# Projecting three units from x split without its norm, with the token factors applied later

## The chip, the cores and the metric

The kernel runs on one NeuronCore of a Trainium2 chip. The metric is the time of one execution on the device in microseconds (us). The kernel before took 1175.54 us (median of 3 runs, 1175.41 to 1177.18).

## What is computed

One step of a hybrid decoder layer on 1088 tokens (1024 of a prompt, 8 times 8 of samples) of width 1024, in float32. Only the first lines matter for this change:

```python
h = rmsnorm(x, norm_mix_pre[l])              # x * rsqrt(mean(x*x) + eps) * g
(a_b, a_c, a_u, b_p, c_q, c_f, c_i, c_g, d_a, d_g) = jnp.split(h @ w_in[l], N_BLOCKS, axis=-1)
...
f = lb + (1.0 - lb) * jax.nn.sigmoid(zf4)    # zf is c_f, q = silu(c_q), v = c_i
...
mix = jnp.concatenate([ya, yb, yc, yd], axis=-1) @ w_out[l]
x = x + rmsnorm(mix, norm_mix_post[l])
```

The norm multiplies each token (a row of x) by one number, r(token) = rsqrt(mean(x*x) + eps), and each channel by a gain g. The factor r can be applied to x ahead of the product with `w_in` or to the product behind it.

## The kernel before, in words

All products run on TensorE as float32 split in two parts: a value is stored as a rounded high part (`xh`, `wop` slot 0) and the remainder (`xl`, `wop` slot 1), and one product is three matmuls: high by high, low x by high weight, high x by low weight. The high part is made by a copy on ScalarE (ACT), the low part by a subtraction on VectorE (DVE) that needs the high part. `XH[k]` and `XL[k]` (k = 0 to 7) hold the normed input, channels of block k on the partitions and the 1088 tokens along the row.

**Units.** The 2560 columns of `w_in` are 20 units of 128 columns. A unit is 8 blocks k times 3 token chunks `CH` (256, 384 and 448 tokens) times 3 matmuls: 72 matmuls into three PSUM banks (`mm`, six banks, so two units at a time). A unit's weights come in two halves of 256 KB (`raw`, 4 buffers), each split into `wop` (4 buffers). `UNITS` is the order of the units; a unit's handler (`c_f`, `c_q`, `c_v`, `d_gate`, ...) evacuates its banks and does the work of its mixer. Unit 10 is the forget gate zf of head pair 0 (`c_f`, sigmoid), unit 8 its query (`c_q`, silu), unit 12 its value (`c_v`); with zf and the query in SBUF the generator `hgrn(0)` can run, a long chain of DVE work with short matmul blocks on TensorE (lines L746, L759, L811 and on).

**The start.** x comes in token-major from `xn`: nine tiles, 128 tokens on the partitions and 1024 channels in the row (in the buffers `ys`, line L213). For a chunk c: ACT squares each tile with a row sum (`x_sq`, L228), DVE makes r from the sums (`x_norm`) and scales the tiles (L68, partly on GpSimd), TensorE transposes them block by block (`x_split`, L249), ACT takes the high part with the gain out of PSUM (L250) and DVE the low part (L71). Units `U0` = 10 and `U1` = 8 run chunk by chunk between these transposes (`mm_part`, L148). This start is written by hand inside a block that keeps the written order on ACT, DVE and TensorE.

**After it.** `unit` (L997) issues the other 18 units, and a budget hook puts the handlers' work between their matmuls: after every 4 or 8 matmuls it lets generators in the lists `first`, `crit` and `bulk` issue instructions until a budget of modelled work is spent. The order of the instructions on TensorE and DVE is therefore fixed when the program is built. `bulk` holds the depthwise convolutions (60 DVE instructions L71 of 128x1024), `first` the evacuations and the splits of the next unit's weights. Then follow the output projection (L1131) and the feed-forward part, which the change does not touch.

A norm by `rsqrt_steps` is 12 small DVE instructions. `bcast` (L189) turns a column of factors into the same row on all 128 partitions, by a transpose on TensorE into PSUM. `ht()` is a 1088-wide scratch tile (six of them), `zt()` one of two others.

Of the kernel before, what the change touches and what calls it, by code (L numbers as in the profile page):

```python
# [52 lines left out]
def body(ctx, tc, xn, xT, win, wout, wgu, wdn, par, con, msk, poolw, s_conv, s_pool, s_hgrn, s_conf,  # L53
# [165 lines left out]
    def x_idx(c):
        o, n = CH[c]  # L220
        return [i for i, (go, gn) in enumerate(GRP) if o <= go < o + n]

    def x_sq(c):
        ss = sst[c]
        for a, i in enumerate(x_idx(c)):
            gn = GRP[i][1]
            junk = ht(D)
            S.activation(junk[:gn], xs[i][:gn], AF.Square, accum_out=ss[:gn, a:a + 1])  # L228
            yield ss

    def x_norm(c, ss):
        idx = x_idx(c)
        args = ss[:, :len(idx)], [P, len(idx)], 1.0 / D, f"x{CH[c][1]}"
        if c == 0:
            r = rsqrt_pow(*args)
        else:
            for r in rsqrt_steps(*args):
                yield
        for a, i in enumerate(idx):
            gn = GRP[i][1]  # L240
            TS(xs[i][:gn], xs[i][:gn], r[:gn, a:a + 1], 0.0, eng=GP if c and a % 2 else V)
            yield

    def x_split(c, k):
        o, n = CH[c]
        ps = T(mmp, [P, 512], "mm") if k % 2 and c < 2 else sm()
        for i in x_idx(c):
            go, gn = GRP[i]
            PE.transpose(ps[:, go - o:go - o + gn], xs[i][:gn, k * P:(k + 1) * P], ident[:gn, :gn])  # L249
        S.activation(XH[k][:, o:o + n], ps[:, :n], AF.Copy, scale=pc("g_mix", k))  # L250
# [2 lines left out]
    with tc.manual_schedule(engines={mybir.EngineType.Activation, mybir.EngineType.DVE, mybir.EngineType.PE}):
        sq = [x_sq(c) for c in range(3)]

        def steps(g, n):
            for _ in range(n):
                next(g, None)

        for ss in sq[0]:  # L260
            pass
        steps(x_norm(0, ss), 99)
        prep_unit(U0)
        next(sq[1])
        ss1 = next(sq[1])
        x_split(0, 0)
        x_split(0, 1)
        next(sq[1])
        n1 = x_norm(1, ss1)
        pu = {u: [T(mmp, [P, 512], "mm")] for u in (U0,)}  # L270
        for k in range(2, KT):
            x_split(0, k)
            steps(n1, 3)
            mm_part(pu[U0], wq[U0], k - 2, 0)
            if k >= 5:
                ss2 = next(sq[2])
        steps(n1, 99)
        next(sq[2])
        n2 = x_norm(2, ss2)
        mm_part(pu[U0], wq[U0], 6, 0)  # L280
        mm_part(pu[U0], wq[U0], 7, 0)
        pu[U0].append(T(mmp, [P, 512], "mm"))
        pu[U1] = [T(mmp, [P, 512], "mm")]
        for k in range(KT):
            x_split(1, k)
            steps(n2, 2)
            if k == 1:
                prep_unit(U1)
            if k >= 2:
                mm_part(pu[U0], wq[U0], k - 2, 1)  # L290
            if k >= 4:
                mm_part(pu[U1], wq[U1], k - 4, 0)
        steps(n2, 99)
        for k in range(4, KT):
            if k >= 6:
                mm_part(pu[U0], wq[U0], k, 1)
            mm_part(pu[U1], wq[U1], k, 0)
        pu[U0].append(T(mmp, [P, 512], "mm"))
        pu[U1].append(T(mmp, [P, 512], "mm"))
        for k in range(KT):  # L300
            x_split(2, k)
            mm_part(pu[U1], wq[U1], k, 1)
            if k >= 2:
                mm_part(pu[U0], wq[U0], k - 2, 2)
        mm_part(pu[U0], wq[U0], 6, 2)
        mm_part(pu[U0], wq[U0], 7, 2)
        pu[U1].append(T(mmp, [P, 512], "mm"))
        load_unit(U2)
        for k in range(KT):
            mm_part(pu[U1], wq[U1], k, 2)  # L310
            if k == 2:
                prep_unit(U2)
# [1580 lines left out]
```

## Time and profile before

| | |
|---|---|
| median of 3 runs | 1175.54 us |
| the profiled execution | 1176.22 us |
| its span, first to last instruction | 1174.4 us |
| TensorE matmuls busy | 1144.4 us (97%) |
| VectorE busy | 880.8 us (75%) |
| ScalarE busy | 454.9 us (39%) |
| start, until unit three begins | 54.7 us |
| end of the projection, unit 20 | 337 us |

The profile is one execution; its span leaves out about 1.8 us of the measured time. Rows of the timeline give the start of an instruction (or of a run of equal ones), its duration and what released it. In groups the number behind the busy time is the mean duration in ns. A matmul's duration covers its way through the array, so back to back matmuls overlap: their cost on the path is the distance of their starts. "PE" is TensorE, "PEclk" the granted clock.

### The profile page before, as it was taken

The numbers are of one execution on the slowest core, as the hardware profiler recorded it, in microseconds if no ns is written. First come the engines' busy times: TensorE is split into PE (matmuls) and PEld (weight loads), VectorE is DVE, ScalarE is ACT, GpSimd is POOL, SyncE is SP. The second block draws the span as 40 slices with busy tenths as digits, with TensorE's granted clock in tenths as the row PEclk, the third lists the DMA queues.
The fourth block names the chain that finished last, engine by engine and source line by source line (L and its number), as shares of the span: only waits on it lengthen the run. The fifth ranks groups of instructions, "written<-read, shape, count | busy, mean of one in ns | idle before, by whom it ended". The sixth has DMA issues, their size and how long they took to land.

```text
span 1174.4 us, 21922 instructions
## 1 busy us (share of the span) xinstructions
PE 1144.4 (97%) x8480; PEld 1111.4 (95%) x8480; DVE 880.8 (75%) x1831; ACT 454.9 (39%) x1006; POOL 109.9 (9%) x174
## 2 busy tenths in 40 slices
PE   5999999999999999999999999999999999999995
PEld 4899899997999999999999999999999999999995
DVE  5478979996775678887667787787676668888776
ACT  7534232243274453442333444444344541123331
POOL 2100000000000000000000000000000222246323
PEclk9999999999999999999999999999999999999997
DMA  8011112211145124022331543453454687853555
GB/s 265 27 37 32 37 39 69 41 37 24 47 143 191 40 74 131 20 74 91 112 113 48 190 156 103 162 171 112 141 186 139 206 281 212 271 169 109 164 103 98
DMA packets 103401, 136.91 MB, mean 117 GB/s; under 512 B 25025, under 2 KB 72257, under 8 KB 103297
## 3 DMA queue, kind: packets, MB, share of 16 engines
q1 hardware_dynamic: 94944, 108.71, 29.5%
q0 software_dynamic: 8352, 26.81, 8.6%
q8 instruction: 66, 1.08, 0.4%
q14 instruction: 39, 0.31, 0.1%
HBM read 94.90 MB, written 40.57 MB: 115 GB/s over the span
## 4 chain that ended last, share of the span: by engine, by line
PE 92%; DVE 3%; DMA 2%; ACT 2%; issue 1%; SPq 0%; POOL 0%; ACTq 0%; DVEq 0%; POOLq 0%
PE p L1403 31%; PE mm L997 18%; PE p L1636 14%; PE p L1131 8%; PE p L1513 6%; PE p L1312 6%; PE mm L148 2%; PE sm L811 2%; DMA y<-xn 1%; DMA hx<-hi 1%; DVE wop L65 1%; PE sm L886 1%; PE p L1097 1%; PE sm L898 0%; PE sm L409 0%
## 5 line engine op out<-in xcount | busy, mean ns | idle before, releaser
L65 DVE TENSOR_TENSOR wop<-raw,wop 128x512 fp32r<-128x512 f32 (+2 forms) x296 | 195.9, 675 | 99.4 <-ACT wop L1020 90.1
L1403 PE MATMUL p<-xh,wop 128*128 128x272 f32 x1216 | 235.2, 288 | 0.6 <-DVE c L65 0.6
L1020 ACT CAST wop<-raw 128x512 fp32r<-128x512 f32 (+1 forms) x240 | 142.0, 604 | 239.3 <-DVE raw L65 120.3
L1403 PEld LDWEIGHTS p<-xh,wop 128*128 128x128 f32 x1216 | 193.3, 188 | 0.8 <-DVE c L65 0.8
L1403 PE MATMUL p<-t,wop 128*128 128x272 f32 x912 | 176.8, 288 | 0.0
L997 PE MATMUL mm<-xh,wop 128*128 128x256 f32 (+2 forms) x864 | 175.9, 331 | 0.0
L1403 PE MATMUL p<-xl,wop 128*128 128x272 f32 x608 | 175.4, 288 | 0.0
L1403 PEld LDWEIGHTS p<-t,wop 128*128 128x128 f32 x912 | 145.3, 189 | 0.0
L997 PEld LDWEIGHTS mm<-xh,wop 128*128 128x128 f32 x864 | 137.9, 188 | 5.7 <-issue 1.1
L1403 PE MATMUL p<-x,wop 128*128 128x272 f32 x456 | 130.8, 287 | 0.0
L1403 PEld LDWEIGHTS p<-xl,wop 128*128 128x128 f32 x608 | 114.4, 188 | 0.0
L1131 PE MATMUL p<-xh,wop 128*128 128x272 f32 x512 | 98.9, 290 | 0.0
L997 PE MATMUL mm<-xl,wop 128*128 128x256 f32 (+2 forms) x432 | 97.5, 333 | 0.0
L1403 PEld LDWEIGHTS p<-x,wop 128*128 128x128 f32 x456 | 86.3, 189 | 0.0
L1636 PE MATMUL p<-xh,wop 128*128 128x272 f32 x456 | 82.2, 289 | 0.0
L1636 PE MATMUL p<-xl,wop 128*128 128x272 f32 x456 | 81.5, 288 | 0.0
L1131 PEld LDWEIGHTS p<-xh,wop 128*128 128x128 f32 x512 | 81.0, 188 | 0.0
L65 DVE TENSOR_TENSOR raw<-raw,raw 128x512 f32<-128x512 f32 (+1 forms) x123 | 71.2, 589 | 10.0 <-DMA raw<-wgu 7.9
L71 DVE SCALAR_TENSOR_TENSOR y<-u,taps,y 128x1024 f32<-128x1024 f32 x60 | 77.0, 1283 | 1.6
L1131 PE MATMUL p<-xl,wop 128*128 128x272 f32 x256 | 73.9, 289 | 1.0 <-DVE xl L65 1.0
L1312 PE MATMUL p<-xh,wop 128*128 128x272 f32 x384 | 74.0, 290 | 0.0
L65 DVE TENSOR_TENSOR t<-p,t 128x272 f32<-128x272 f32 (+3 forms) x138 | 60.6, 450 | 15.9 <-PE p L1636 8.2
(323 smaller groups left out, 1997.9 us busy)
## 6 DMA issues: line engine op xcount, KB each, us to landing
raw<-wgu SPq DMA_DIRECT2D x88, 256.0 KB, 3.0
hx<-hi SPq DMA_DIRECT2D x84, 136.0 KB, 2.3
raw<-win SPq DMA_DIRECT2D x40, 256.0 KB, 2.9
hx<-x SPq DMA_DIRECT2D x64, 136.0 KB, 2.5
raw<-wdn SPq DMA_DIRECT2D x32, 256.0 KB, 3.6
xh<-hx POOLq DMA_DIRECT2D x15, 544.0 KB, 5.0
xl<-hx POOLq DMA_DIRECT2D x15, 544.0 KB, 5.2
x<-hx POOLq DMA_DIRECT2D x12, 544.0 KB, 5.0
```

Source lines behind the costliest of these rows:

```text
L65: (eng or V).tensor_tensor(out, a, b, op)
L71: (eng or V).scalar_tensor_tensor(out=out, in0=a, scalar=s, in1=b, op0=op0, op1=op1)
L148: PE.matmul(ps[c][:, :n], hl[:, wi, kk], X[k][:, o:o + n], start=k == 0 and wi == 0 and X is XH, stop=k == KT - 1 and wi == 1)
L811: PE.matmul(ps[:rows, g * P:(g + 1) * P], kk[:, o:o + rows], qz[hf][:, :, g * 64:(g + 1) * 64], start=True, stop=True, skip_group_check=True)
L886: PE.matmul(op[hs, :gn], v[:gn, g, hs], attn[:gn, g, h, :gn], start=True, stop=g == 0, skip_group_check=True)
L997: PE.matmul(ps[c][:, :w], hl[:, wi, kk], X[k][:, o:o + w], start=k == order[0] and wi == 0 and X is XH, stop=k == order[-1] and wi == 1)
L1020: S.copy(hl[:, 0], raw)
L1131: PE.matmul(ps[nt][:, :PW], WO[nt][k // 4][:, wi, kk:kk + P], X[k][:, o:o + PW], start=k == korder[0] and wi == 0 and X is XH, stop=k == k ...
L1312: PE.matmul(ps[r][:, :PW], w[:, wi, (k % 4) * P:(k % 4 + 1) * P], X[k][:, o:o + PW], start=k == 0 and wi == 0 and X is XH, stop=k == KT - ...
L1403: PE.matmul(ps[:, :PW], wop[:, wi, kk * P:(kk + 1) * P], x(kk, xi), start=first and kk == 0 and wi == 0 and xi == 0, stop=kk == 3 and wi == 1,
L1513: PE.matmul(ps[:, :n], wd[:, wi, kk * P:(kk + 1) * P], hops[k][xi][:, o:o + n], start=first and kk == 0 and wi == 0 and xi == 0, stop=not ...
L1636: PE.matmul(ps[:, :PW], ws[name][wi][q], x[:, xi, pr], start=first and q == 0 and wi == 0 and xi == 0, stop=q == 1 and wi == 1, skip_group ...
```

## The change

- x is loaded once, already transposed (`xT`, channels on the partitions), straight into `ys`; `xn`, all transposes of x and the three norms by chunk are gone.
- First split: for each k, `XH[k]` and `XL[k]` are made from x times the gain alone, in one piece of 1088 tokens (k = 0 in three), without r. The three first units (12, 10, 8 now: value, forget gate, query) run on these. Unit 12's matmuls for block k follow that block's split; those of unit 10 follow three blocks behind.
- The squares (ACT) are added up over k on DVE; nine matmuls with a column of ones give the sums per token, `rsqrt_steps` gives `r0`, and nine `bcast` with three copies give `rb0`, r spread over all partitions.
- r is applied at evacuation: unit 12 is copied out as it is and its transposed value gets r as the scale of the ACT copy (nine copies where there were three); units 10 and 8 are multiplied by `rb0` on DVE before sigmoid and silu.
- Second split, ahead of unit four (18): for each k DVE scales x in place by gain and `rb0`, ACT copies it to `XH[k]`, DVE subtracts to `XL[k]`. The other 17 units use these.
- `hgrn(0)` starts with unit four; the value's handler starts from the copy `zv`.

The diff, cut to its core:

```diff
-    UNITS = (10, 8, 12, 18, 16, 13, 19, 11, 9, 17, 4, 2, 6, 0, 5, 3, 7, 1, 14, 15)
-    U0, U1, U2 = UNITS[:3]
-    xs = [ys[i][:, :D] for i in range(KT)] + [ht(D)]
...
-                SY.dma_start(xs[i][:gn], xn[go:go + gn, :])
...
-            PE.transpose(ps[:, go - o:go - o + gn], xs[i][:gn, k * P:(k + 1) * P], ident[:gn, :gn])
-        S.activation(XH[k][:, o:o + n], ps[:, :n], AF.Copy, scale=pc("g_mix", k))
-        STT(XL[k][:, o:o + n], ps[:, :n], pc("g_mix", k), f32(XH[k][:, o:o + n]), ALU.mult, ALU.subtract)
...
+    UNITS = (12, 10, 8, 18, 16, 13, 19, 11, 9, 17, 4, 2, 6, 0, 5, 3, 7, 1, 14, 15)
+    U0, U1, U2, U3 = UNITS[:4]
+    for k in range(KT):
+        if k in (0, 2):
+            load_unit(U0 if k == 0 else U1)
+        SY.dma_start(ys[k], xT[k * P:(k + 1) * P, :])
+    load_unit(U2)
+    def split_x(k, scale, parts):
+        for o, n in parts:
+            if scale is None:
+                S.copy(XH[k][:, o:o + n], ys[k][:, o:o + n])
+                TT(XL[k][:, o:o + n], ys[k][:, o:o + n], f32(XH[k][:, o:o + n]), ALU.subtract)
+            else:
+                S.activation(XH[k][:, o:o + n], ys[k][:, o:o + n], AF.Copy, scale=scale)
+                STT(XL[k][:, o:o + n], ys[k][:, o:o + n], scale, f32(XH[k][:, o:o + n]), ALU.mult, ALU.subtract)
+    def mm_unit(n, *ks):
+        for k in ks:
+            for c in range(len(CH)):
+                mm_part(pu[n], wq[n], k, c)
...
+        prep_half(U0, 0)
+        for k in range(KT):
+            split_x(k, pc("g_mix", k), CH if k == 0 else [(0, NT)])
+            if k == 0:
+                prep_half(U0, 1)
+            if k in (2, 3):
+                prep_half(U1, k - 2)
+            sq[k] = ht(NT)
+            S.activation(sq[k], ys[k], AF.Square)
+            mm_unit(U0, k)
+            if k >= 3:
+                mm_unit(U1, k - 3)
+            if k == 1:
+                acc0 = sq[0]
+            if k >= 1:
+                TT(acc0, acc0, sq[k], ALU.add)
+        zv.append(zt())
+        for c, (o, n) in enumerate(CH):
+            S.copy(zv[0][:, o:o + n], pu[U0][c][:, :n])
+        mm_unit(U1, 5)
...
+            PE.matmul(st[:gn, i:i + 1], acc0[:, go:go + gn], ones[:, :1], start=True, stop=True, skip_group_check=True)
+        mm_unit(U1, 6)
+        for r0 in rsqrt_steps(st[:, :9], [P, 9], 1.0 / D, "x"):
             pass
+        prep_half(U2, 0)
+        prep_half(U2, 1)
+        load_unit(U3)
+        mm_unit(U1, 7)
...
+                    bcast(ps, r0[:, i:i + 1], gn, go - o)
+            S.copy(rb0[:, o:o + n], ps[:, :n])
+            mm_unit(U2, c)
+        HF[0] = ht()
+        for c, (o, n) in enumerate(CH):
+            TT(HF[0][:, o:o + n], pu[U1][c][:, :n], rb0[:, o:o + n])
+        S.activation(HF[0], HF[0], AF.Sigmoid)
+        mm_unit(U2, *range(3, KT))
+        prep_half(U3, 0)
+        prep_half(U3, 1)
         for k in range(KT):
+            STT(ys[k], ys[k], pc("g_mix", k), rb0, ALU.mult, ALU.mult)
+            split_x(k, None, [(0, NT)])
+            if k == 3:
+                HQ[0] = ht()
+                for c, (o, n) in enumerate(CH):
+                    TT(HQ[0][:, o:o + n], pu[U2][c][:, :n], rb0[:, o:o + n])
+                S.activation(HQ[0], HQ[0], AF.Silu)
...
-    free = {"h": 6, "z": 2, "u": 2, "sm": 2, "mm": 0, "v": 1, "attn": 1}
+    free = {"h": 4, "z": 1, "u": 2, "sm": 2, "mm": 6, "v": 1, "attn": 1}
...
-            S.copy(v[:n2, i:i + m], t[:n2, :m * P].rearrange("p (m c) -> p m c", c=P))
+            if ps is None:
+                for i2 in range(i, i + m):
+                    S.activation(v[:n2, i2], t[:n2, (i2 - i) * P:(i2 - i + 1) * P], AF.Copy, scale=r0[:n2, i2:i2 + 1])
+            else:
+                S.copy(v[:n2, i:i + m], t[:n2, :m * P].rearrange("p (m c) -> p m c", c=P))
```

How the instructions stand, at the two places that matter below. First DVE, where before the last chunk of x is split behind its transposes (`xl` is the low part, `sm` a transposed block in PSUM, `prm` the gains; number behind xl, xh and y is k), and behind it the splits of units two and three (`wop`):

```order
L71 SCALAR_TENSOR_TENSOR xl4_18_92<-sm_90_431,prm_1_70,xh4_10_84 128x448
L71 SCALAR_TENSOR_TENSOR xl5_19_93<-sm_91_444,prm_1_70,xh5_11_85 128x448
L71 SCALAR_TENSOR_TENSOR xl6_20_94<-sm_92_457,prm_1_70,xh6_12_86 128x448
L71 SCALAR_TENSOR_TENSOR xl7_21_95<-sm_93_470,prm_1_70,xh7_13_87 128x448
L65 TENSOR_TENSOR wop_97_503<-raw_95_490,wop_97_503 128x512
L65 TENSOR_TENSOR wop_98_506<-raw_96_492,wop_98_506 128x512
```

In the change DVE has this ahead of and in unit four, the second split (`y` is x, `h_71` is `rb0`):

```order
L65 TENSOR_TENSOR wop_76_485<-raw_66_376,wop_76_485 128x512
L65 TENSOR_TENSOR wop_77_488<-raw_67_378,wop_77_488 128x512
L71 SCALAR_TENSOR_TENSOR y0_22_102<-y0_22_102,prm_1_70,h_71_392 128x1088
L65 TENSOR_TENSOR xl0_14_88<-y0_22_102,xh0_6_80 128x1088
L71 SCALAR_TENSOR_TENSOR y1_23_103<-y1_23_103,prm_1_70,h_71_392 128x1088
L65 TENSOR_TENSOR xl1_15_89<-y1_23_103,xh1_7_81 128x1088
```

One instruction of a block moved to two, the low part standing directly behind the scaling of the same block; between the two ACT makes `xh` of that block.

Second DVE, where before `hgrn(0)` begins (`h_107` is the forget gate, `h_108` the query), while unit three runs:

```order
L68 TENSOR_SCALAR h_107_543<-h_107_543 128x1088
L65 TENSOR_TENSOR wop_115_580<-raw_112_554,wop_115_580 128x512
L65 TENSOR_TENSOR wop_116_586<-raw_113_556,wop_116_586 128x512
L723 RECIPROCAL h_117_595<-h_107_543 128x128x2
L725 RECIPROCAL h_117_595<-h_107_543 128x128
L71 SCALAR_TENSOR_TENSOR h_117_595<-h_108_547,h_117_595 128x128
```

In the change the same instructions (`h_75` the forget gate, `h_78` the query) stand among the second split of blocks 4 to 7, while unit four runs:

```order
L71 SCALAR_TENSOR_TENSOR y4_26_106<-y4_26_106,prm_1_70,h_71_392 128x1088
L68 TENSOR_SCALAR h_75_435<-h_75_435 128x1088
L65 TENSOR_TENSOR wop_96_587<-raw_90_542,wop_96_587 128x512
L65 TENSOR_TENSOR wop_97_590<-raw_91_544,wop_97_590 128x512
L715 RECIPROCAL h_99_599<-h_75_435 128x128x2
L65 TENSOR_TENSOR xl4_18_92<-y4_26_106,xh4_10_84 128x1088
L71 SCALAR_TENSOR_TENSOR y5_27_107<-y5_27_107,prm_1_70,h_71_392 128x1088
L717 RECIPROCAL h_99_599<-h_75_435 128x128
```

`hgrn(0)` moved from unit three to unit four, and its pieces now stand ahead of the low parts that unit four's matmuls need. On TensorE the blocks of `hgrn(0)` stand about 0.9 of a unit later at first, and from the tenth unit on the order is that of before.

More of the change, by code (lines that the diff above doesn't have):

```diff
@@ L50, with body @@
 NCON = 174
-def body(ctx, tc, xn, xT, win, wout, wgu, wdn, par, con, msk, poolw, s_conv, s_pool, s_hgrn, s_conf,
+def body(ctx, tc, xT, win, wout, wgu, wdn, par, con, msk, poolw, s_conv, s_pool, s_hgrn, s_conf,
          yT, o_conv_p, o_pool_p, o_hgrn_p, o_conf_p, o_conv_s, o_pool_s, o_hgrn_s, o_conf_s, hd, hx):
@@ L219, in x_idx @@
[L219 to L250, printed above, removed]
-        STT(XL[k][:, o:o + n], ps[:, :n], pc("g_mix", k), f32(XH[k][:, o:o + n]), ALU.mult, ALU.subtract)
[L253 to L260, printed above, removed]
-            pass
[L262 to L283, printed above, removed]
-        for k in range(KT):
[L285 to L312, printed above, removed]
@@ new lines, in mm_unit, with banks, prep_half @@
+    def mm_unit(n, *ks):
+        for k in ks:
+            for c in range(len(CH)):
+                mm_part(pu[n], wq[n], k, c)
+    def banks():
+        return [T(mmp, [P, 512], "mm") for _ in CH]
+    def prep_half(n, h):
+        hl = T(wp, [P, 2, 4 * P], "wop", F32R).rearrange("p w (k c) -> p w k c", c=P)
+        split_w(wraw[n][h], hl)
+        wq.setdefault(n, []).append(hl)
+    pu = {}
+    HF, HQ, zv = {}, {}, []
+    with tc.manual_schedule(engines={mybir.EngineType.Activation, mybir.EngineType.DVE, mybir.EngineType.PE}):
+        sq, acc0 = {}, None
+        pu[U0], pu[U1] = banks(), banks()
+        prep_half(U0, 0)
[18 more added lines that the diff above has]
+        mm_unit(U1, 5)
+        st = sm()
+        V.memset(st[64:, 8:9], 1.0)
+        for i, (go, gn) in enumerate(GRP):
+            PE.matmul(st[:gn, i:i + 1], acc0[:, go:go + gn], ones[:, :1], start=True, stop=True, skip_group_check=True)
+        mm_unit(U1, 6)
+        for r0 in rsqrt_steps(st[:, :9], [P, 9], 1.0 / D, "x"):
+            pass
+        prep_half(U2, 0)
+        prep_half(U2, 1)
+        load_unit(U3)
+        mm_unit(U1, 7)
+        pu[U2] = banks()
+        rb0 = ht(NT)
+        for c, (o, n) in enumerate(CH):
+            ps = sm()
+            for i, (go, gn) in enumerate(GRP):
+                if o <= go < o + n:
+                    bcast(ps, r0[:, i:i + 1], gn, go - o)
[8 more added lines that the diff above has]
+        prep_half(U3, 1)
+        for k in range(KT):
+            STT(ys[k], ys[k], pc("g_mix", k), rb0, ALU.mult, ALU.mult)
+            split_x(k, None, [(0, NT)])
+            if k == 3:
+                HQ[0] = ht()
+                for c, (o, n) in enumerate(CH):
+                    TT(HQ[0][:, o:o + n], pu[U2][c][:, :n], rb0[:, o:o + n])
+                S.activation(HQ[0], HQ[0], AF.Silu)
@@ L677, in c_v @@
     def c_v(j, ps):
-        yield from take(z=1)
-        z = zt()
-        evac(ps, z)
-        give(mm=3)
+        if ps is None:
+            z = zv[0]
+        else:
+            yield from take(z=1)
+            z = zt()
+            evac(ps, z)
+            give(mm=3)
         yield from wait(2 * LW)
@@ L693, in c_v @@
             n2 = GRP[i][1]
[L694 removed]
+            if ps is None:
+                for i2 in range(i, i + m):
+                    S.activation(v[:n2, i2], t[:n2, (i2 - i) * P:(i2 - i + 1) * P], AF.Copy, scale=r0[:n2, i2:i2 + 1])
+            else:
+                S.copy(v[:n2, i:i + m], t[:n2, :m * P].rearrange("p (m c) -> p m c", c=P))
             give(sm=1)
@@ L1053, in body @@
             if n in pu:
-                first.append(handler(j, pu[n]))
-                if i == 1:
-                    until(lambda: free["mm"] >= 3)
+                if n == U0:
+                    first.append(c_v(0, None))
+                elif n == U2:
+                    crit.append(hgrn(0))
                 continue
@@ L1871 @@
     wdn = c(a["w_down"][0].reshape(NF, P, KT, P).transpose(2, 1, 0, 3))
-    ins = {"xn": c(x), "xT": c(x.T), "win": units(a["w_in"][0]), "wout": units(a["w_out"][0]), "wgu": wgu, "wdn": wdn,
+    ins = {"xT": c(x.T), "win": units(a["w_in"][0]), "wout": units(a["w_out"][0]), "wgu": wgu, "wdn": wdn,
            "par": c(np.concatenate(par, axis=1)),
```

8 lines of the change are left out of this document (1 added, 7 removed).

## The prediction

> **What bounds the kernel now.** First the page, then TensorE's (PE's) waits, then the windows.
>
> ```profile
> span 1174.4 us, 21922 instructions
> PE 1144.4 (97%) x8480; PEld 1111.4 (95%) x8480; DVE 880.8 (75%) x1831; ACT 454.9 (39%) x1006; POOL 109.9 (9%) x174
> ```
> ```profile
> PE sm L249 <- DVE y L68: 10.5, 2, 10.3
> PE mm L148 <- ACT xh L250: 2.1, 3, 1.5
> ```
> ```profile
> 0.00:54.70 54.70, 39.85 (x217) 34.16 (x218) 26.19 (x70) 35.21 (x61) 9.23 (x16) 1.00 0.46 152
> 54.70:81.60 26.90, 26.90 (x186) 24.99 (x185) 18.32 (x35) 8.74 (x14) 0.00 (x0) 1.00 0.12 40
> 81.60:100.00 18.40, 18.40 (x126) 17.70 (x125) 12.78 (x26) 7.93 (x18) 0.00 (x0) 1.00 0.09 29
> 100.00:120.00 20.00, 20.00 (x137) 19.13 (x136) 18.82 (x31) 10.36 (x27) 0.00 (x0) 1.00 0.15 34
> 120.00:140.00 20.00, 20.00 (x134) 17.83 (x133) 18.14 (x22) 6.23 (x22) 0.00 (x0) 1.00 0.16 54
> 140.00:160.00 20.00, 20.00 (x137) 18.20 (x136) 19.38 (x24) 6.83 (x18) 0.00 (x0) 1.00 0.10 29
> 160.00:180.00 20.00, 20.00 (x133) 19.10 (x132) 13.51 (x24) 4.04 (x7) 0.10 (x1) 1.00 0.13 28
> ```
>
> PE is the bound: its columns are full from 54.7 on. Only the start lacks work for it: 14.9 of 54.7 us idle, 10.3 of that until the first transpose. In a part where PE is always busy, time can only be lost, by making PE wait; so I ask when PE comes to one and the same point, the start of unit five (16), and what it and DVE still owe there. DVE is third in row (columns: length, PE, weight loads, DVE, ACT): from 100 to 160 it is busy 56.3 of 60 us, so work pushed into that stretch has little room.
>
> Rows of PE's timeline give the prices of its work:
>
> ```profile
> 16.54 0.41 PE L148 MATMUL mm<-xl,wop 128*128 128x256 f32 x1
> 16.75 0.41 PE L148 MATMUL mm<-xh,wop 128*128 128x256 f32 x1
> ...
> 18.87 0.28 PE L148 MATMUL mm<-xh,wop 128*128 128x256 f32 x1
> 18.99 0.38 PE L249 MATMUL mm<-cst,y 128*128 128x128 f32 x2
> ...
> 29.05 0.49 PE L249 MATMUL sm<-cst,y 128*128 128x128 f32 x3
> 29.30 0.42 PE L148 MATMUL mm<-xh,wop 128*128 128x384 f32 x1
> ...
> 55.15 0.66 PE L997 MATMUL mm<-xl,wop 128*128 128x256 f32 x3
> ...
> 56.63 0.65 PE L997 MATMUL mm<-xl,wop 128*128 128x256 f32 x3
> ...
> 65.61 1.16 PE L746 MATMUL sm<-h 64*128 64x128 f32 x16
> 66.70 0.76 PE L997 MATMUL mm<-xl,wop 128*128 128x256 f32 x3
> ```
>
> A block k of a unit (nine matmuls) takes 56.63 - 55.15 = 1.48 us, a unit 11.84; three transposes 0.25; a block of `hgrn(0)` (L746) 1.09. Until 18.9 a 256-wide matmul takes 0.21 from start to start, then 0.12: PE begins at about half speed.
>
> The other engines' prices, by shape:
>
> ```profile
> L65 DVE TENSOR_TENSOR xl<-y,xh 128x1088 fp32r<-128x1088 f32 x7 | 9.0, 1292 | 0.9 <-ACT xh L1043 0.8
> L71 DVE SCALAR_TENSOR_TENSOR y<-u,taps,y 128x1024 f32<-128x1024 f32 x60 | 77.0, 1283 | 1.6
> L65 DVE TENSOR_TENSOR wop<-raw,wop 128x512 fp32r<-128x512 f32 x248 | 168.2, 692 | 87.9 <-ACT wop L1020 80.7 <-ACT wop L141 6.2
> L65 DVE TENSOR_TENSOR u<-mm,z 128x384 f32<-128x384 f32 x8 | 4.0, 545 | 0.0
> L751 DVE COPY_PREDICATED attn<-mk,sm 128x512 f32<-128x512 uint32 x8 | 5.5, 737 | 8.5 <-PE sm L746 8.5
> L68 DVE TENSOR_SCALAR y<-y,rs_x256y 128x1024 f32<-128x1024 f32 x2 | 1.4, 750 | 0.8 <-POOL rs_x256y L131 0.8
> ```
> ```profile
> L1043 ACT CAST xh<-y 128x1088 fp32r<-128x1088 f32 x7 | 7.7, 1107 | 2.0 <-PE mm L997 2.0
> L228 ACT ACTIVATE h<-y 128x1024 f32<-128x1024 f32 x8 | 8.4, 1054 | 3.7 <-DMA y<-xn 3.6
> L141 ACT CAST wop<-raw 128x512 fp32r<-128x512 f32 x40 | 24.8, 622 | 62.8 <-PE mm L997 55.4 <-issue 5.6 <-PE mm L148 1.0
> L449 ACT ACT_TABLE_LOAD x6 | 7.7, 1283 | 0.1
> ```
> ```profile
> L409 PE MATMUL sm<-ones,h 128*128 128x1 f32 x18 | 2.3, 245 | 0.0
> ```
> ```profile
> 55.46 0.73 DVE L68 TENSOR_SCALAR h<-h 128x1088 f32<-128x1088 f32 x1 [4.22 <-ACT h L710]
> ...
> 58.44 1.75 DVE L723 RECIPROCAL h<-h 128x256 f32<-128x256 f32 x1
> 60.10 0.90 DVE L725 RECIPROCAL h<-h 128x128 f32<-128x128 f32 x1
> ...
> 63.27 0.39 DVE L71 SCALAR_TENSOR_TENSOR h<-h,h 128x128 f32<-128x128 f32 x1
> ```
>
> The first half of `hgrn(0)`'s first step is 5.2 us of DVE (58.44 to 63.66); back to back the next instruction starts 0.09 before the end of the one before.
>
> **Part by part, on the profiled execution's clock.** *Loading.* ACT's first squares and weight copies wait for landings:
>
> ```profile
> 5.56 1.06 ACT L228 ACTIVATE h<-y 128x1024 f32<-128x1024 f32 x1 [2.35 <-DMA y<-xn]
> ...
> 7.29 1.06 ACT L228 ACTIVATE h<-y 128x1024 f32<-128x1024 f32 x1 [0.59 <-DMA y<-xn]
> ...
> 8.93 1.28 ACT L141 CAST wop<-raw 128x512 fp32r<-128x512 f32 x2 [0.49 <-DMA raw<-win]
> ...
> 10.88 1.06 ACT L228 ACTIVATE h<-y 128x1024 f32<-128x1024 f32 x1 [0.67 <-DMA y<-xn]
> ```
>
> Each half megabyte takes 1.6 to 2.0 us. The change asks for weights first, then x block 0: about 5.6 and 7.4; later blocks come at least every 2.0 us. Masks and states now queue on SP behind weight loads that wait for a free buffer; they are wanted some 60 us later, so this costs nothing. GpSimd loses its scalings, which nobody here waits for.
>
> *First split.* Block 0 (three pieces) is done on DVE at 9.6; ACT copies a weight half (0.62), squares (1.12) and makes the next high part (1.11): 11.6, and the low part (1283 x 1088/1024 = 1.36) is there at 12.9. From then on DVE sets the step, low part and sum of squares 1.36 + 1.29 - 0.16 = 2.5, with 0.6 more for a weight half in blocks 2 and 3: low parts at 15.4, 18.5 (block 3), 21.6, ..., 29.1 (block 7). PE waits for block 3, then has 13 blocks of units 12 and 10 (19.2) and the nine sums (18 matmuls, 2.3): it ends unit 10 at 40.0. The square root chain (12 small DVE instructions) lies under two of these blocks. Nine transposes (0.75) and unit 8: its end is 52.6.
>
> *Factors and evacuation.* The last copy of `rb0` ends about 44.3 (two blocks, nine transposes, 0.6). Behind it ACT loads the sigmoid table (1.28), runs the sigmoid (1.2, an estimate from the 1.11 of a copy), copies two weight halves (0.62 + 0.53), DVE splits the last (0.69): 48.6.
>
> *Second split.* DVE has for each block scaling, then low part, and ACT's copy between them, so nothing overlaps: 1.36 + 1.11 + 1.29 + 0.06 for two handovers - 0.09 = 3.7. Four blocks: 63.6. The query's three products (0.40 + 0.55 + 0.61 - 0.2, from the 384-wide row by width) 65.0. Then, as the order shows, scaling 1.3, forget gate 0.64, two weight halves 1.2, reciprocal 1.66 ahead of low part 4: 71.0; then scaling 5 (1.3), the rest of that half of `hgrn(0)` 3.6, low parts 5 and 6 (2.4), scalings 6 and 7 (2.6), two masked copies 1.4, low part 7 (1.3): 83.5. PE needs 0.98 more for its last six matmuls: unit five starts at **84.5**. PE has 13.7 us of work from 52.6 on and waits the other 18.
>
> *Before, the same point.* 54.66 + 2 x 11.84 + two blocks of L746 (2.2) + nine transposes (0.75) + a small block (0.26) = **81.6**. So PE is 2.9 late and owes the second block and the small one, 1.35: 4.3.
>
> *Debt of DVE.* At this point DVE owes the second half of that step, its masks and first products, about 9 us that it had done before; PE's owed 1.35 pays part. The idle time before from 81.6 to 180 is 5.6 + 1.2 + 1.9 + 0.6 + 6.5 = 15.8, enough in sum, but 3.7 in the dense 60 us. No stall to all 7.6 of it are possible; walking through the order, PE's matmuls stay ahead by 0 to 4 us of what they wait for, so I take 0.7, near the lower end.
>
> From unit ten on the order is the same and nothing else changes. Sum: 2.9 + 1.35 + 0.7 = +5.0, by the profiled execution 1176.2 to 1181.2 us; it lay 0.7 above the median, so **1180.5** against 1175.54.
>
> *A rule about the clock.* The cold rows above warm up 8.6 us after PE's first matmul (10.3 to 18.9). [...] The trace's start agrees with half speed; no row here shows a fall after a pause. [...]
>
> **Rivals.** *Shorter links (0.20).* The chain of the second split is 35 us long; were its links 7% shorter (1.20 instead of 1.29, as starts back to back are), and DVE's debt free, 2.4 + 0.7 go: +1.9, 1177.4, within 0.2% (2.35 us, about what a measurement of this kernel can tell). For it: the 0.09 of overlap in every row. Against it: an engine that waits for another has no overlap.
>
> *The clock falls (0.10).* Blocks 4 to 7 still fit their waits at half speed; the last six matmuls take 0.8 longer, and a start like the first is cold for up to 8.6 us, losing up to 3.9: +4.7, 1185.2. It decides if a pause above 4 us is enough. Against it: PE's pauses of 10 us apart, no row. [...]
>
> *DVE's debt stalls PE (0.07).* In units six to ten all 7.6 instead of 0.7: 1187.4. It decides where the walk finds PE less than 1 us behind DVE. For it: 56.3 of 60 us busy. Against it: DVE's order there was drawn up again around the later `hgrn(0)`.
>
> *Faster: DVE at the rate of L68 (0.12).* That row scales 1024 columns in 0.75. If DVE's work on x, all from SBUF now, ran so, 1088 columns take 0.8: links of 2.7 for 3.7 (-4.2 over four blocks), eight instructions behind them 0.5 shorter (-4.0), the first split paced by ACT (-1.4): +5.0 - 9.6, 1170.9. It decides if two-tensor work takes below 0.9. Against it: 1292 ns for just this subtraction. The chance is above what these rows leave, since it stands also for a pace of landing or handover that no row shows.
>
> **How the numbers follow.** The forecast has 0.51, from +2.4 to +8 (1178 to 1183.5). Slower by over 0.2%: 0.51 + 0.10 + 0.07 = 0.68; within: 0.20; faster: 0.12. The range leaves out the faster case and the full debt: 1173 to 1186.
>
> **What would show it.** In the profile after: unit 8 ends near 52.6; PE waits some 18 us on `xl<-y,xh` and `xh<-y` between 50 and 85; DVE alternates 1.3 us of scaling, 1.1 idle, 1.3 of low part; unit five starts near 84.5. Wrong if DVE does not idle there (links), if matmuls behind 84 take 0.41 (clock), if PE waits on DVE between 100 and 180 (debt), or if PE has no waits behind 55 at all.

## The result, and the profile after

The changed kernel takes 1186.81 us (median of 4 runs, 1185.16 to 1187.87); the kernel before, beside it, 1176.36 (4 runs, 1175.41 to 1179.23). The ratio is 1.0083, with a 95% interval of 1.0061 to 1.0106: slower by 10 us. The forecast was 1180.5 and its range ended at 1186. The profiled execution took 1185.16 us, the fastest of the four, with a span of 1182.8; before it was 1176.22 and 1174.4. So the two profiles can account for 8.9 of the 10.4 us.

The page of the changed kernel, span and busy time:

```profile
span 1182.8 us, 21814 instructions
PE 1145.1 (97%) x8435; PEld 1108.7 (94%) x8435; DVE 902.6 (76%) x1827; ACT 457.1 (39%) x993; POOL 104.9 (9%) x170
```

DVE has 22 us more to do than before (880.8), and PE stands idle for 37.7 us where it was 30.0. Its waits (total, times, longest):

```profile
PE mm L148 <- ACT xh L222: 10.6, 2, 10.3
PE mm L989 <- ACT xh L219: 6.9, 6, 4.1
PE mm L148 <- DVE xl L71: 3.0, 3, 1.3
...
PE mm L989 <- DVE xl L65: 1.0, 3, 0.5
```

The second and fourth row are unit four (L989 on the second split). They hold 7.9 us, not the 18 that were forecast; the windows say why (columns: length, PE, weight loads, DVE, ACT, GpSimd, granted clock, share and GB/s of the DMA engines):

```profile
54.70:85.00 30.30, 22.21 (x91) 16.20 (x91) 26.34 (x34) 15.14 (x22) 0.00 (x0) 0.73 0.05 18
...
140.00:160.00 20.00, 19.94 (x134) 17.25 (x132) 17.45 (x25) 7.29 (x23) 0.00 (x0) 1.00 0.08 27
160.00:180.00 20.00, 19.79 (x132) 18.30 (x133) 19.02 (x29) 6.84 (x18) 0.56 (x1) 1.00 0.13 29
```

PE is busy for 22.2 of the 30.3 us with only 91 matmuls, at a mean clock of 0.73: it worked at half speed for a large part of its waiting time, so the waits look shorter than they are. Between 100 and 180, where DVE's debt was feared, PE idles 0.27 us.

The second split on DVE, from its timeline (start, duration, what it waited for), and the end of unit four on PE:

```profile
53.73 1.29 DVE L65 TENSOR_TENSOR xl<-y,xh 128x1088 fp32r<-128x1088 f32 x1 [1.17 <-ACT xh L219]
54.94 1.35 DVE L71 SCALAR_TENSOR_TENSOR y<-y,prm,h 128x1088 f32<-128x1088 f32 x1
57.45 1.29 DVE L65 TENSOR_TENSOR xl<-y,xh 128x1088 fp32r<-128x1088 f32 x1 [1.17 <-ACT xh L219]
...
84.95 1.28 DVE L65 TENSOR_TENSOR xl<-y,xh 128x1088 fp32r<-128x1088 f32 x1
```
```profile
72.53 1.28 PE L989 MATMUL mm<-xh,wop 128*128 128x256 f32 x3 [4.12 <-ACT xh L219]
...
81.52 2.08 PE L738 MATMUL sm<-h 64*128 64x128 f32 x16
...
86.28 0.77 PE L989 MATMUL mm<-xl,wop 128*128 128x256 f32 x3
86.89 1.15 PE L989 MATMUL mm<-xh,wop 128*128 128x256 f32 x6
```

A link is 57.45 - 53.73 = 3.72 us. The last low part is done at 86.2; of the six matmuls at 86.89 three end unit four and three begin unit five, at 87.4. Unit four lasts 32.1 us (from 55.3) for the 13.7 us of work that the forecast gave it: 18.4 are lost. Before, the same point is in this row, whose last three matmuls begin unit five, at 82.4:

```profile
81.87 1.15 PE L997 MATMUL mm<-xh,wop 128*128 128x256 f32 x6
```

So unit five is 5.0 us late. Much later, in unit ten, the same products of `hgrn(0)` stand in both kernels, one row of each:

```profile
201.94 1.16 PE L746 MATMUL sm<-h 64*128 64x128 f32 x16
```
```profile
209.12 1.16 PE L738 MATMUL sm<-h 64*128 64x128 f32 x16
```

7.2 us late: the 2.2 since unit five are work that the kernel before had done by then, but for 0.27 of idle time. The output projection starts 7.3 late (336.9, 344.2), the last part of the feed-forward 9.1 late (1085.6, 1094.7), the end is 8.4 late.

### The profile page after: what moved, and what is told of

The parts are those of the page before. It is cut to its first block, busy times and chain, and to the rows that moved or that the text cites. A ratio compares the mean times of both kernels' runs of the same rounds, so it can differ in the third digit from the quotient of the medians.

```text
span 1182.8 us, 21814 instructions
## 1 busy us (share of the span) xinstructions
PE 1145.1 (97%) x8435; PEld 1108.7 (94%) x8435; DVE 902.6 (76%) x1827; ACT 457.1 (39%) x993; POOL 104.9 (9%) x170
## 4 chain that ended last, share of the span: by engine, by line
PE 88%; DVE 7%; ACT 2%; DMA 1%; issue 1%; SPq 0%; POOL 0%; DVEq 0%; ACTq 0%; POOLq 0%
PE p L1396 30%; PE mm L989 16%; PE p L1629 14%; PE p L1124 8%; PE p L1305 6%; PE p L1506 6%; PE mm L148 3%; PE sm L803 2%; DVE wop L65 1%; DVE y L71 1%; DVE xl L65 1%; DVE raw L65 1%; DMA raw<-wgu 1%; DMA y<-xT 1%; PE p L1090 1%
## 5 line engine op out<-in xcount | busy, mean ns | idle before, releaser
L989 PE MATMUL mm<-xh,wop 128*128 128x256 f32 (+2 forms) x816 | 172.8, 338 | 6.9 <-ACT xh L219 6.9
L989 PEld LDWEIGHTS mm<-xh,wop 128*128 128x128 f32 x816 | 132.4, 192 | 15.1 <-ACT xh L219 9.5
L989 PE MATMUL mm<-xl,wop 128*128 128x256 f32 (+2 forms) x408 | 94.7, 341 | 1.3 <-DVE xl L65 1.0
L989 PEld LDWEIGHTS mm<-xl,wop 128*128 128x128 f32 x408 | 66.5, 192 | 7.4 <-DVE xl L65 3.9
```

Of the source, the lines that this page charges most:

```text
L989: PE.matmul(ps[c][:, :w], hl[:, wi, kk], X[k][:, o:o + w], start=k == order[0] and wi == 0 and X is XH, stop=k == order[-1] and wi == 1)
```

## Experiments

Theory A: the chain of the second split on DVE sets the end of unit four, and it started late because block 0 of x landed late. Theory B: the halved clock is what costs. Theory C: part of the loss is made behind the projection. Theory D came up with the first runs: the clock falls to half for short stretches, at places that vary from execution to execution. Each run has the median, and the ratio to the kernel before with its 95% interval; the changed kernel stands at 1.0083.

**x_first.**

```diff
     for k in range(KT):
+        SY.dma_start(ys[k], xT[k * P:(k + 1) * P, :])
         if k in (0, 2):
             load_unit(U0 if k == 0 else U1)
-        SY.dma_start(ys[k], xT[k * P:(k + 1) * P, :])
...
-        prep_half(U0, 0)
         for k in range(KT):
             split_x(k, pc("g_mix", k), CH if k == 0 else [(0, NT)])
             if k == 0:
+                prep_half(U0, 0)
                 prep_half(U0, 1)
```

> Block 0 of x asked for ahead of the first unit's weights, and its high parts ahead of the copy of the weights on ACT. Theory A (the late landing of block 0, 9.8 instead of 7.4, is the missing term): block 0 lands near 5.6, PE's first matmul starts 1.5 to 2.5 us earlier than 10.3, every later step of the start with it, unit four starts near 53 instead of 55.4, and the time falls by 1.5 to 3 us, to about 1184.5. Rival: what is won at the first block is lost again, since the weights land later by as much and blocks 1 to 3 are paced by landing: no change of more than 0.7 us.

ACT's first high part, in the changed kernel and in this one:

```profile
9.78 1.57 ACT L222 ACTIVATE xh<-y,prm 128x256 fp32r<-128x256 f32 x3 [3.46 <-DMA y<-xT]
```
```profile
5.93 1.57 ACT L222 ACTIVATE xh<-y,prm 128x256 fp32r<-128x256 f32 x3 [2.72 <-DMA y<-xT]
```

Block 0 lands 3.9 us earlier, PE's first matmul starts at 8.06 instead of 10.34, unit four at 52.6 instead of 55.3 (the forecast had 52.6), and the last products of the second hgrn stage (L738) end 3.1 earlier, at 206.9. Each step is as theory A has it. Yet the profiled execution takes 1185.78, the median is 1185.59 (1182.04 to 1187.36; ratio 1.0073, 1.0059 to 1.0087): only 1.2 gained, less than expected and not clear of the noise. The 3.1 us were lost again in one place:

```profile
308.60:312.00 3.40, 3.40 (x31) 3.37 (x30) 1.13 (x2) 0.00 (x0) 0.00 (x0) 0.99 0.43 72
312.00:318.80 6.80, 6.80 (x25) 6.53 (x25) 5.19 (x28) 0.62 (x1) 0.00 (x0) 0.50 0.01 2
318.80:322.20 3.40, 3.40 (x17) 2.66 (x16) 0.87 (x2) 2.16 (x4) 0.00 (x0) 1.00 0.51 154
```

For 6.8 us the clock is at half, in a part where PE never waits: 3.4 us lost. The changed kernel's own profile has no fall there. This is what gave theory D.

**keep_warm.**

```diff
+    zero = T(const, [P, 64], "zero", F32R)
+    S.activation(zero, ones[:, :64], AF.Copy, scale=0.0)
...
                 if wi == 1:
                     reached[0] += n == UNITS[-1]
+                    for _ in range((6, 6, 6, 16, 10, 10, 6, 0)[k] if n == U3 else 0):
+                        PE.matmul(ps[2][:64, :448], zero, XH[0][:, 640:NT], start=False, stop=False)
```

> Matmuls with zero weights, added to unit four's sums where PE waits, hold PE busy: 60 of them, no other change. Theory A: the granted clock stays 1.00 from 54.7 to 85, the mean clock of the run rises to about 0.995, but low part 7 comes when it did (86.2), so the time is that of the changed kernel, 1186.8, within 0.7 us. Theory B: with the clock at full speed the time falls by 3 to 5 us, to 1182 to 1184.

```profile
54.70:85.00 30.30, 27.18 (x156) 20.63 (x155) 26.21 (x32) 14.43 (x22) 0.00 (x0) 1.00 0.06 20
```

The clock stays at 1.00 (mean of the run 0.995). 1185.7 us (ratio 1.0078, 1.0064 to 1.0091), not to be told from the changed kernel. In the profiled execution unit four started 1.4 late (56.7, behind a fall at 40.3) and the second hgrn stage 0.8 late: by these two profiles full clock in unit four is worth some 0.6 us. Theory B falls: 17 us at half clock cost next to nothing, since PE was waiting for DVE and ACT anyway.

**scale_ahead.**

```diff
+        STT(ys[0], ys[0], pc("g_mix", 0), rb0, ALU.mult, ALU.mult)
         for k in range(KT):
-            STT(ys[k], ys[k], pc("g_mix", k), rb0, ALU.mult, ALU.mult)
-            split_x(k, None, [(0, NT)])
+            S.copy(XH[k], ys[k])
+            if k + 1 < KT:
+                STT(ys[k + 1], ys[k + 1], pc("g_mix", k + 1), rb0, ALU.mult, ALU.mult)
+            TT(XL[k], ys[k], f32(XH[k]), ALU.subtract)
```

> Second split with the scaling of block k+1 ahead of the low part of block k on DVE. Theory A (the chain of the second split sets the end of unit four): DVE's four pauses of 1.17 us in blocks 0 to 3 go, low parts come every 2.5 us instead of 3.72, unit five starts near 83 instead of 87.4, the time falls by 3.5 to 5.5 us from the changed kernel's 1186.8, to about 1182.3. Theory B (the halved clock behind 65 us is what costs): PE still waits in unit four, so the clock still falls and the time stays above 1185. Theory C (the loss is made behind the projection): no change of more than 1 us.

DVE's pauses go, low parts come every 2.46 us, unit five starts near 82.5. But two new waits appear:

```profile
PE mm L992 <- ACT xh L292: 4.1, 1, 4.1
PE sm L741 <- DVE h L71: 3.8, 1, 3.8
```

The scheduler now puts hgrn(0)'s pieces on DVE behind the low parts, and PE, whose order has their products in the middle of unit four, stands there for 3.8 us. The second hgrn stage is 3.3 earlier than in the changed kernel; the profiled execution takes 1182.81, the median 1186.58 (1182.81 to 1187.87; ratio 1.0081, 1.0066 to 1.0095). The steps came, the median did not: the five others ran at mean clocks of 0.984 to 0.988, the profiled one at 0.990. They were 3.0 to 5.1 us longer, and 0.002 to 0.006 of 1183 us is 2.4 to 7.1; that falls of the clock are what they lost is likely by that, but none of the five was traced.

**no_second_split.**

```diff
         for k in range(KT):
-            STT(ys[k], ys[k], pc("g_mix", k), rb0, ALU.mult, ALU.mult)
-            split_x(k, None, [(0, NT)])
```

> Leaves out the second scaling and split altogether, so that units four to twenty work on x without its token factor. Theory A: PE runs through unit four without a wait, from 55.4 on it stands 0.7 us behind the kernel before and DVE has no more to do than there: about 1177, 9 to 10 us below the changed kernel; the second split is the whole loss but 0.7. Theory C (part of the loss, 1.5 to 3 us, comes from behind the projection or from the first split): 1179 to 1181.

The kernel leaves out the second split, so its results are not those of the layer; it serves for the time alone. 1169.29 us (ratio 0.9942, 0.9924 to 0.9960), 8 below what I expected of it. I had forgotten that at 55 us the changed kernel has three units done and the kernel before two; a unit is 11.84. The output projection starts at 327.8, 9.1 earlier than before. So the second split costs 17.5 us in all, and without it the change would gain 7. Theory C is not the main cause, though 1.1 us are lost there too (see the points below).

**changed_again.** No edit.

> The changed kernel itself, unaltered, run again for its spread. Theory D (TensorE's clock falls to half for whole stretches of 3.4 us behind a stretch in which its columns were idle more than about half, and which stretches those are depends on where the grid of stretches falls in this execution): median 1186.8 within 0.6, executions spread over 3 us or more, slower ones at a lower mean clock (0.984 against 0.988), and in the profile falls of 3.4 us or multiples of it at other places than in the first profile. Rival (one fixed length): executions within 1 us.

1186.85 us (1184.75 to 1190.52; ratio 1.0084, 1.0064 to 1.0103); the spread is 5.8 us. This time the profile is of an execution of 1187.87, 2.7 more than the first. It has two falls that the first has not:

```profile
36.70:40.10 3.40, 3.40 (x28) 3.35 (x27) 1.02 (x7) 0.00 (x0) 0.00 (x0) 1.00 0.00 0
40.10:43.50 3.40, 3.40 (x13) 3.08 (x12) 2.08 (x8) 0.00 (x0) 0.00 (x0) 0.50 0.13 36
...
84.50:87.90 3.40, 1.71 (x10) 1.13 (x8) 3.40 (x5) 2.38 (x2) 0.00 (x0) 1.00 0.00 0
87.90:91.30 3.40, 3.40 (x13) 3.24 (x12) 3.37 (x7) 1.75 (x4) 0.00 (x0) 0.50 0.02 5
```

Each takes about 1.7 us from PE where PE is the bound: unit four starts at 56.5 instead of 55.3, the second hgrn stage is 2.5 late, the end 2.7. That is theory D, and it fits that the first profile, without these two falls, lies below the median. The mean clock of the two profiled executions is the same, 0.988: where a fall lies decides what it costs.

**early_split** (on top of x_first).

```diff
+        STT(ys[0], ys[0], pc("g_mix", 0), rb0, ALU.mult, ALU.mult)
-        S.activation(HF[0], HF[0], AF.Sigmoid)
         mm_unit(U2, *range(3, KT))
-        prep_half(U3, 0)
-        prep_half(U3, 1)
         for k in range(KT):
...
+            if k < 2:
+                prep_half(U3, k)
+            if k == 1:
+                S.activation(HF[0], HF[0], AF.Sigmoid)
-            if k == 3:
+            if k == 7:
                 HQ[0] = ht()
```

> Block 0 of x first, second split straight behind the token factors (ahead of the sigmoid and of unit four's weights), the scaling of block k+1 ahead of the low part of block k, the query's products behind the last block. Theory A: first low part near 49 instead of 55, one every 2.6 us, the last near 68 instead of 86, unit five starts near 70 instead of 87.4; behind that DVE is busy without a break to about 170, so PE gets back some waits there: the projection ends 12 us earlier than in the changed kernel, the time is 1172 to 1177, at or below the kernel before (1176.7). Rival (DVE's whole work until 170 is the bound, and the order in which it is done changes nothing): 1182 or more, with PE's waits moved behind 70.

```profile
57.71 1.34 DVE L71 SCALAR_TENSOR_TENSOR y<-y,prm,h 128x1088 f32<-128x1088 f32 x1
58.97 1.28 DVE L65 TENSOR_TENSOR xl<-y,xh 128x1088 fp32r<-128x1088 f32 x1
60.17 1.34 DVE L71 SCALAR_TENSOR_TENSOR y<-y,prm,h 128x1088 f32<-128x1088 f32 x1
```
```profile
74.75 2.08 PE L746 MATMUL sm<-h 64*128 64x128 f32 x16 [10.22 <-DVE h L71]
```

DVE runs without a gap, a low part every 2.47, the last at 66.4. PE does not wait for x any more, but for 10.2 us for hgrn(0)'s first half, which DVE reaches only then. 1181.09 us (1177.1 to 1183.94, 12 runs; ratio 1.0029, 1.0015 to 1.0042): 6 below the changed kernel, 3 above the kernel before, between the two theories. (The fastest of the twelve lists a mean clock of 0.942, all others 0.985 to 0.989; so the mean clock alone doesn't tell a slow execution.)

**early_pool.**

```diff
+            if k in (1, 3, 5, 7):
+                GP.tensor_tensor(ys[k], ys[k], rb0, ALU.mult)
+            else:
                 STT(ys[k], ys[k], pc("g_mix", k), rb0, ALU.mult, ALU.mult)
```

> As early_split, but blocks 1, 3, 5 and 7 are scaled by their token factors on GpSimd instead of DVE (gains folded into the two split instructions). Theory A: DVE has 5 us less to do in the stretch that bounds, so 2 to 5 us below early_split, 1168 to 1174, if a scaling takes GpSimd 2.5 us or less and DVE's rows keep their 1.3 us. Rival: the two engines slow each other, DVE's rows of 1.3 grow while GpSimd runs or GpSimd's scalings take over 4 us: the same as early_split or slower.

GpSimd's four scalings, and DVE's rows beside and behind them:

```profile
44.73 12.57 POOL L289 TENSOR_TENSOR y<-y,h 128x1088 f32<-128x1088 f32 x4 [40.44 <-ACT h L281]
```
```profile
45.22 3.20 DVE L71 SCALAR_TENSOR_TENSOR y<-y,prm,h 128x1088 f32<-128x1088 f32 x1
...
51.91 3.03 DVE L65 TENSOR_TENSOR wop<-raw,wop 128x512 fp32r<-128x512 f32 x1
54.86 3.59 DVE L71 SCALAR_TENSOR_TENSOR y<-y,prm,h 128x1088 f32<-128x1088 f32 x1
58.37 1.34 DVE L71 SCALAR_TENSOR_TENSOR xl<-y,prm,xh 128x1088 fp32r<-128x1088 f32 x1
```

A scaling takes GpSimd 3.1 us, and until 57.3 DVE's scaling takes 3.2 to 3.6 instead of 1.34, a weight split 3.03 instead of 0.68. The rival holds: 1186.47 us (ratio 1.0075, 1.0058 to 1.0093), 5.4 above early_split. DVE's instructions above are 1.9 to 2.4 us longer beside GpSimd's scalings than behind them (3.20 and 3.59 against 1.34, 3.03 against 0.68); why, no run shows.

**early_spread** (on top of early_split).

```diff
+            if i in (2, 5):
+                mm_unit(U1, 4 + i // 3)
...
-            if k >= 3:
+            if 3 <= k < 7:
                 mm_unit(U1, k - 3)
```

> As early_split, with the nine one-column sums on PE spread in threes between blocks of the second unit instead of standing together. Theory D: no fall of the clock behind the sums (as seen at 40.3 us in two of four profiles), so the median is 0 to 1.2 us below early_split and the executions lie closer. Rival (the falls have nothing to do with the sums): the same as early_split within 0.7.

1180.93 us (1176.74 to 1183.34, 12 runs; ratio 1.0028, 1.0014 to 1.0041), the same as early_split and no narrower: no verdict. The falls that remain (66.9, 309 and here 900) lie elsewhere.

**late_hgrn, mid_hgrn, mid_late_hgrn** (on top of early_spread): hgrn(0) is started behind unit four, in its middle, or after three quarters of it. The diff is that of mid_hgrn, cut; mid_late_hgrn has 12 in place of 8, and late_hgrn appends hgrn(0) behind unit four's `drive` and handler.

```diff
-                elif n == U2:
-                    crit.append(hgrn(0))
...
-            drive(unit(n, ps))
+            products = unit(n, ps)
+            if n == U3:
+                for _ in range(8):
+                    hook(next(products) * MM)
+                crit.append(hgrn(0))
+            drive(products)
```

The three expectations, in that order:

> As early_spread, and hgrn(0) is started behind unit four's matmuls instead of ahead of them, so that its first matmuls on PE stand a unit later. Theory A (in early_split PE stood 10.2 us at these matmuls because DVE reached that half only then): the wait of 10.2 shrinks below 4 us, unit five starts near 67 and runs, the projection ends 5 to 8 us earlier than in early_split (340.8 in its profile): 1172 to 1176. Rival (DVE is the bound until 170 in any order): the wait turns up as waits of other matmuls for DVE between 70 and 180, and the time stays at 1180 or above.

> As early_spread, with hgrn(0) started in the middle of unit four: its first matmuls on PE stand half a unit (6 us) later than in early_spread, half a unit earlier than in late_hgrn. If the place in PE's order was what cost in early_spread: the wait of 10.2 us there falls to about 4, DVE's idle time between 70 and 100 (7.7 us in early_split) to about 3, and the time falls by 3 to 5 us from early_spread's 1180.9, to 1176 to 1178. If DVE's own chain through both hgrn stages is the bound (late_hgrn, where 10 us of PE's waits went and came back at the projection's end): the same as early_spread within 1.5 us, with the second hgrn stage no earlier than 203.

> The same, started after three quarters of unit four. If the place in PE's order was what cost: no wait left at hgrn's first matmuls, 1175 to 1178. If DVE's chain is the bound: PE's last projection matmul ends earlier than in early_spread (340.5), PE waits by as much for the high and low parts of the next stage's input, and the time is that of early_spread or of late_hgrn, 1180 to 1183.

late_hgrn's wait at these products is 0.2 us, its last projection matmul is issued at 330.1, 10.7 earlier than in early_split, and then PE stands at the output projection for the last mixers' results:

```profile
PE p L1133 <- ACT xh L1044: 3.3, 1, 3.3
...
PE p L1133 <- DVE xl L65: 2.3, 7, 0.9
```

1182.35 us (ratio 1.0068, 1.0044 to 1.0093). mid_hgrn:

```profile
PE p L1136 <- DVE xl L65: 3.4, 3, 2.3
PE sm L747 <- DVE h L71: 3.0, 1, 3.0
```

1176.66 us (1175.06 to 1179.64, 12 runs; ratio 0.9999, 0.9987 to 1.0010), 10 below the changed kernel and the same as the kernel before. Its projection's last matmul is issued at 328.8, 7.9 earlier than in the kernel before, but 4.6 of that gain go in the output projection, in waits for the mixers' results and one stretch of half clock behind them (from 335.4 to 338.8): the products behind it start at 436.1, against 439.4 before. Another 2.4 go in the 400 us of feed-forward products (402.4 against 400.0), 1.4 of them in a longer wait for DVE. mid_late_hgrn takes 1183.06 (ratio 1.0050, 1.0034 to 1.0065). So the place in PE's order was what made PE wait in early_spread, but all three places bring back, as waits at the projection's end, part of what they free in unit five, and two of them all of it: the order of DVE's work through both hgrn stages decides too. Why the middle is so much better than three quarters stays open; three points don't tell it.

**late_spread, before_spread.** The sums of the mixers' norms (18 small matmuls each) are let in singly between blocks instead of in threes, on top of late_hgrn and of the kernel before.

```diff
             pe(0.22)
-            if i % SP == SP - 1:
-                yield None
+            yield None
```

> As late_hgrn, and the one- and two-column sums of the mixers' statistics stand singly between blocks instead of in threes. Theory D: the fall of the clock near 308 to 318 us is gone, 0 to 3.3 us below late_hgrn in the median and with executions closer together. Rival: the falls have another cause, the same as late_hgrn within 0.7.

> The kernel before, with only this spreading of the statistics' sums. Its executions so far fall into two groups, 1174.7 to 1176.6 at a mean clock of 0.995 and 1177.9 to 1179.9 at 0.992 or 0.993. Theory D (the second group has one fall of two stretches, 6.8 us, in the last unit, where small sums fill PE): all executions at a clock of 0.995 and a time of 1174.5 to 1176.7. Rival: still two groups 3 us apart.

Both missed. late_spread takes 1185.98 (ratio 1.0079, 1.0061 to 1.0096), before_spread 1188.85 (1.0109, 1.0096 to 1.0122), with falls still at 312 to 320 and, behind new waits at the projection's end, at 336 to 353 (late_spread) and 348 to 355 (before_spread). The edit moved more than the sums, so it doesn't tell whether they alone make the fall there. That the kernel before has its two groups of executions (0.995 and 0.992 to 0.993, some 3 us apart) from a fall of 6.8 us fits the numbers (0.0025 of 1178 us is 5.9 us at half clock), but no profile caught one: not shown.

## Why the prediction was wrong, point by point

The direction and the mechanism were right, the size was too small by 5.4 us. By profiles, the forecast of +5.0 stands against 8.9. Of the 5.4, 2.3 come from the start, where block 0 of x landed 2.4 late, 1.1 from behind the projection, 0.5 from outside the span and 1.5 from what lies between the profiled execution and the median:

| step | forecast | measured |
|---|---|---|
| block 0 of x has landed | 7.4 | 9.8 |
| low part of block 3, first split | 18.5 | 20.9 |
| unit 8 (third unit) ends | 52.6 | 55.3 |
| weight splits done, second split can start | 48.6 | 51.2 |
| link of the second split | 3.7 | 3.72 |
| low part 7 | 83.5 | 86.2 |
| unit five starts | 84.5 | 87.4 |
| unit five starts before | 81.6 | 82.4 |
| unit five is late by | 2.9 | 5.0 |
| owed by PE, and stall by DVE's debt | 1.35 + 0.7 | 2.2, of which 0.27 stall |
| late at the projection's end | 5.0 | 7.3 |
| behind the projection | 0 | +1.1, and 0.5 outside the span |

- **The step that failed** is the loading: "The change asks for weights first, then x block 0: about 5.6 and 7.4." I had taken 1.6 to 2.0 us per half megabyte from the landings before, and set x straight behind the first half of the weights. But two halves of 256 KB are asked for ahead of x, and in the trace the first landed at 5.67, the second at 7.48 and x at 9.69: a weight half took as long as I had given a block of x twice its size. All the rest of the start hangs on it, so the 2.4 us go on through the further steps, whose own prices were right to 0.1 to 0.3. x_first shows it in the profile: with x asked for first, unit four starts at the forecast's 52.6. In the median its gain was only 1.2.
- **The same point before** was added up to 81.6 and is 82.4: PE's matmuls stand further apart around a block of other work (the six ahead of `hgrn(0)`'s block at 65.61 take 1.09 instead of 0.99, the three behind it 0.59 instead of 0.49), six such blocks stand there, and the sum had nothing for that. Part of this error comes back with the other sign: PE owes some 1.9 at unit five and not 1.35.
- **From the profile to the median** the forecast took off 0.7 (the profiled execution of before was that much above the median of the runs shown); the profiled execution of the changed kernel lay 1.65 below its median. changed_again shows what the others have: more falls of the clock, at places that vary.
- **Behind the projection** I had nothing, since nothing else changes there. Between 336.9 and 1174.4 the changed kernel loses 1.1 us more. The profile shows waits for DVE of 0.45 at 487 and 0.22 at 1082. The greatest part comes evenly over the first 3192 feed-forward products, of which the first and last start stand in these rows:

```profile
L1403 PE MATMUL p<-xh,wop x1216: 283/288/393, 516.5 to 916.5; 128*128 128x272 f32 x174
```
```profile
L1396 PE MATMUL p<-xh,wop x1216: 283/288/392, 524.4 to 925.4; 128*128 128x272 f32 x174
```

  They take 401.0 us instead of 400.0 at full clock, with one wait of 0.6 in each. Without pauses the mean distance of two starts is 125.1 ns in the profiles of before and before_spread and 125.4 in all thirteen of kernels with the change. So it belongs to the changed program; why, no run shows.
- **Rival "the clock falls"** happened, but cost some 0.6 and not up to 4.7. The clock went to half at 65.07 already, ahead of the pause of 4.1 us at 68.4 that was its condition; behind that pause, from 71.90 on, it was at half as the rival had it, and it was full again at 85.55, ahead of unit five. The part "Blocks 4 to 7 still fit their waits at half speed" was right. The rival's 1185.2 lies near the measured time by chance.
- **Rival "shorter links"**: the links were 3.72. **Rival "DVE's debt"**: 0.27 of 7.6. **Rival "faster"**: two-tensor instructions stayed at 1.29 and 1.35.
- "PE waits some 18 us on `xl<-y,xh` and `xh<-y`" was wrong as an observation: the waits read 7.9, because PE filled the rest at half speed. What stood behind it was right: unit four lost 18.4 us, and without the second split the whole kernel is 17.5 us shorter.

## What to carry to other kernels

A chain's first landing carries through everything behind it: price it from a landing in the same place of the queue with the same bytes ahead, and ask first for what the longest chain needs (3.9 us at the landing here, though only 1.2 in the median and not clear of the noise). Two engines that hand a tile to and fro cost their sum (3.72 us a block) unless the next tile's first step stands ahead of this tile's last (2.47); and when that is mended, look in the in-order queue for the next instruction that was placed by the old timing (here 10.2 us). When a kernel's executions differ by more than an edit is worth, compare where their stretches of half clock lie, and not the mean clock alone, before believing a difference.
